# Room, order and place of loads, block inverses and output weights around a gated-delta-rule loop

## The chip, the cores and the metric

The kernel runs on one core of a Trainium2 chip, in one launch, all in float32 (products on the TensorE are taken as three products of split operands, high by high, high by low and low by high). The metric is the device time in microseconds (us) of one execution; less is better. Engines are called PE (TensorE), DVE (VectorE), ACT (ScalarE), POOL (GpSimd) and SP (SyncE, which here only issues DMAs).

## The reference

One layer of a hybrid decoder trunk, 1024 positions, width 1024. The mixer runs three branches on one projection of the normed input, and its output goes through `w_out`; cross attention to a memory of 256 rows and an MLP follow:

```
h = rms_norm(x, norm_mix); proj = h @ w_in
qkv, z, a_g, b_g, c_q, c_kv, k_idx, w_idx, ug = split_cols(proj, IN_SPLITS)
y_a = gdn_mixer(qkv, z, a_g, b_g, ...)      # conv over 4 taps, silu, gated delta rule, norm * silu(z)
y_b = dsa_mixer(c_q, c_kv, k_idx, w_idx, ...)  # index scores, top 256 of them, attention on these
y_c = conv_mixer(ug, ...)                   # depthwise conv over 31 taps, layer norm, silu
x = x + concat([y_a, y_b, y_c]) @ w_out
x = x + memory_cross_attention(rms_norm(x), rms_norm(mem), ...)
x = x + square(relu(rms_norm(x) @ w1)) @ w2
```

The gated delta rule is computed in chunks. For each chunk a unit lower triangular matrix I + A is inverted (`triangular_solve` in the reference); then a scan over the chunks carries a state S: `v_new = u - w S`, `o = q S + (qk) v_new`, `S = S * decay + k^T v_new`.

## The kernel before

**How the order comes about.** The program is written as Python generators that are woven together by weights (`weave`, line 65): each `yield` names a cost, and the thread that has had the least of its share is asked next. From the program and a model of durations a planner then fixes one list of instructions for each engine and each DMA queue ahead of the run. On the chip each engine and each queue works through its own list strictly in order; semaphores hold an instruction until its inputs are there and its room is free. Tiles lie in pools that are stacked from the left or the right end of the on-chip memory; a tile in a new pool waits until the last reader of what lay there is done.

**Stages.** (1) Norm, small projections, index scores. (2) `qkv_stage` (line 721) makes the q, k, v channels in 12 blocks of 128; each block's two halves are copied from PSUM by ACT, then convolved over four taps and stored to `qkv_d`. Woven into it are the search for the 256th score (`topk`: ACT and DVE count scores against a threshold, 32 rounds) and the first part of the 31-tap convolution on PE. (3) The preparation: `gdn_pre` (line 907) for chunks 0 to 7 of 128 positions makes the matrices and stores them to `gp_d`; `gdn_blocks(pool, n)` (line 980) inverts the 16 x 16 diagonal blocks of four chunks at a time on DVE, from `Ab_d` to `Xb_d`; `gdn_post` (line 1023) builds the full inverse from them on PE. It runs for chunks 0 to 3 and 4 to 7, the first call woven into the preparation and the second last in it. Beside it run the memory's norm, the K/V projection of the memory (`mem_stage`, whose results go to `kT_d` and `v_d`), the end of the search and of the convolution.

(4) The loop over chunks n = 0 to 7 (lines 1666 to 1694): `gdn_scan(n)` (stage name `gs`), `gdn_post(n + 1)` (`gi`) and a slice of `dsa_out` (`da`, `wa`), the attention on the selected positions and its part of `w_out`, are woven. `gdn_load` (line 895) brings a chunk's five matrices from HBM into a pool with two buffers, on the left; ahead of the first of these loads the program asks for KA and VS, keys and values of the attention. The weights `woa` of the attention's and convolution's rows of `w_out` are loaded raw into `Pm` slots, split by ACT and by DVE or POOL (`big_w_steps`, line 1221), one in each of the first four of 19 items of `dsa_out`.

(5) After the loop `out_rows` and `out_b` (`wb`) add the scan's rows of `w_out` (the weights `wb`, loaded here by the same helper into slots of `blk2`, which is opened here), `cross_q` and the rest follow (`xq`, `xp`, `xv`, `xw`), then the MLP.

**Rooms before.** On the right, in the loop: `pm` (probabilities and raw weights), `woa`, `gdnb` (the scan's `vn`, `S` and its output tiles `oc`). On the left: `gdnc` (what the inverses need), `gdnl` (the loop's loads), `dsa`. After the loop `blk` begins on the left, `blk2`, `xl` and others on the right, over these.

Of the kernel before, what the change touches and what calls it, by code (L numbers as in the profile page):

```python
# [32 lines left out]
P = 128  # L33
T = 1024
# [16 lines left out]
class Block:  # L51
# [187 lines left out]
    def mem_stage(self, wu, mp):  # L239
# [12 lines left out]
        def keys(g):  # L252
            pt = self.mm_ps([P, 2, 2, P])
            for h in range(2):
                for t in range(2):
                    nc.tensor.transpose(pt[:, h, t], kn[g][:, t, h], self.ident)
            kt = [mp.tile([P, 2, 256], F32R, name=f"kvt{i}") for i in range(2)]
            self.split(kt[0], kt[1], pt.rearrange("p h t c -> p h (t c)"))
            for i in range(2):
                nc.sync.dma_start(self.kT_d[i, :, 2 * g:2 * g + 2], kt[i].bitcast(F32))  # L260

        for g in range(4):
# [24 lines left out]
            else:  # L287
# [3 lines left out]
                for i in range(2):  # L291
                    nc.sync.dma_start(self.v_d[i, :, :, (g - 2) * 256:(g - 1) * 256], vt[i].bitcast(F32))
            if g >= 2:
# [428 lines left out]
    def qkv_stage(self, wu, wp, hT):  # L722
# [14 lines left out]
        for i in range(12):  # L737
# [7 lines left out]
            acc = wp.tile([P, T], F32, name="acc", bufs=2)  # L745
            tmp = wp.tile([P, T], F32, name="xtap", bufs=1)
            for d, x, j in ((acc, xb[:, 3:], 3), (tmp, xb[:, 0:T], 0)):
                nc.scalar.activation(d, x, AF.Copy, scale=self.cw[:, j, i:i + 1])
            nc.gpsimd.tensor_add(acc, acc, tmp)
            for d in range(1, 3):  # L750
                nc.vector.scalar_tensor_tensor(acc, xb[:, 3 - d:3 - d + T], self.cw[:, 3 - d, i:i + 1], acc,  # L751
                                               op0=OP.mult, op1=OP.add)
# [142 lines left out]
    def gdn_load(self, pool, n, c):  # L895

        for i, nm in enumerate(("vb", "kd", "qE", "qkT")):
            c[nm] = pool.tile([P, H, P], F32, name="l" + nm, bufs=2)
            self.nc.sync.dma_start(c[nm].rearrange("p h c -> p (h c)"), self.gp_d[n, i])
        c["kT"] = pool.tile([P, H, P], F32, name="lkT", bufs=2)  # L900
        self.nc.sync.dma_start(c["kT"], self.qkv_d[n, :, H:2 * H, :])
# [295 lines left out]
    def dsa_out(self, dp, pmp, wap, KA, VS, NEGM, wa, fw):  # L1197
# [3 lines left out]
        for i in range(len(items) + 3):  # L1201
# [6 lines left out]
            yield from self.weave(*ths)  # L1208
            if i < 4:
                next(fw)  # L1210
# [51 lines left out]
    def out_load(self, pool, t):  # L1262
        ya = pool.tile([P, 512], F32, name="yai", bufs=2)
        gz = pool.tile([P, H, P], F32, name="gz", bufs=2)
        q = self.nc.gpsimd if t < 2 else self.nc.sync
        q.dma_start(ya, self.ya_d[t])
        self.row_load = q.dma_start(gz, self.gz_d[t])
        return ya, gz
# [309 lines left out]
    def run(self):  # L1578
# [85 lines left out]
        ts.close()  # L1664
        wus.close()
        with ExitStack() as bs:
# [12 lines left out]
            wout = A["w_out"][0].rearrange("(k p) n -> p k n", p=P)  # L1679
            wa = []  # L1680
# [18 lines left out]
        with ExitStack() as bs:  # L1699
# [9 lines left out]
            oT, h3, y3 = {}, {}, {}  # L1709
            blk2 = bs.enter_context(sb_pool(tc, "blk2", bufs=4, side="right"))  # L1710

            def slot2(name="wslot"):
                return blk2.tile([P, 2, 1024], F32R, name=name, tag="blk2")

# [4 lines left out]
            with ExitStack() as xs:  # L1719
                xas = xs.enter_context(ExitStack())  # L1720
                xl = xas.enter_context(sb_pool(tc, "xl", bufs=1, side="right"))
                xbs = xas.enter_context(ExitStack())
                self.xt, xe, wr, xq = (xbs.enter_context(sb_pool(tc, x, bufs=1, side="right")) for x in ("xt", "xe", "wr", "xq"))
                xp = xl
                self.xl, self.xq = xl, xq
                def raw():
                    return wr.tile([P, 1024], F32, name="wraw", bufs=2)

# [15 lines left out]

                g2 = xp.tile([P, D], F32, name="g2")
                rows = {i: self.out_load(xe, i) for i in range(2)}
                nc.sync.dma_start(g2, bass.AP(tensor=A["norm_cross"].tensor, offset=A["norm_cross"].offset, ap=[[0, P], [1, D]]))
                wb, wq = [], []
# [14 lines left out]
                for i in range(NT + 6):  # L1763
# [18 lines left out]
                    if i == 9:  # L1782
                        wo = self.big_w(slot2, raw2, A["xa_wo"][0].rearrange("(k p) n -> p k n", p=P), H, D)
                        g3 = xp.tile([P, D], F32, name="g3", tag="g2")
                        nc.sync.dma_start(g3, bass.AP(tensor=A["norm_mlp"].tensor, offset=A["norm_mlp"].offset, ap=[[0, P], [1, D]]))
# [66 lines left out]
```

## Time and profile before

| | us |
|---|---|
| median of 3 runs | 1598.34 (1595.43 to 1599.29) |
| profiled execution | 1596.08 |
| its span | 1594.30 |
| PE busy | 1500.4 |
| DVE busy | 1113.8 |
| ACT busy | 739.3 |
| POOL busy | 286.0 |

The span goes from the first to the last instruction. The mean granted clock of PE is 0.973 of full speed. In the 40 slices of the page PE shows 9 (90% or more) nearly everywhere; the slices below 8 are the first one (6), the one from 359 to 399 us (7) and the one from 518 to 558 us (4). Busy times say how long an engine works, not whether anyone waits for it; that is read from the waits, the order of time and the stretches.

### The profile page before, as it was taken

Reading aid. Unit: us, or ns where it says so; the run is one execution under the profiler, and the core shown is the slowest. Engines: PE = TensorE matmul, PEld = TensorE weight load, DVE = VectorE, ACT = ScalarE, POOL = GpSimd, SP = SyncE. Lnnn points to the kernel's source line nnn. Section 1 sums busy time; section 2 is a strip of 40 time slices with the busy share of each in tenths; the row PEclk is TensorE's granted clock in tenths of the full one; section 3 lists DMA queues with packets and bytes.
Section 4 is the critical chain, followed back from the end, with each engine's and each line's share of the span. In section 5 each row is a group of like instructions: output and inputs, shape, how many; then the busy total and the mean of one; then the engine's idle time right before and its main releaser. Section 6 shows DMA issues by size and latency. Waiting matters only on the chain.

```text
span 1594.3 us, 20703 instructions
## 1 busy us (share of the span) xinstructions
PE 1500.4 (94%) x7561; PEld 1257.0 (79%) x7561; DVE 1113.8 (70%) x2056; ACT 739.3 (46%) x1381; POOL 286.0 (18%) x270
## 2 busy tenths in 40 slices
PE   6999999997999489999889998999999999999999
PEld 5977887786888378988668886888888888888887
DVE  6648667875655666775557779996579647865783
ACT  4535788768543165674334533532233233313331
POOL 4021444343953231121300200000000000000000
PEclk9999999999999799999999999999999999999999
DMA  6130222122474675434712347923641464147202
GB/s 212 38 106 14 56 84 79 54 66 75 148 250 148 224 255 163 143 104 143 257 67 67 119 172 277 361 80 131 233 171 53 158 224 163 36 158 264 79 13 94
DMA packets 125141, 220.82 MB, mean 139 GB/s; under 512 B 16246, under 2 KB 65135, under 8 KB 117871
## 3 DMA queue, kind: packets, MB, share of 16 engines
q1 hardware_dynamic: 123502, 214.25, 39.0%
q0 software_dynamic: 1536, 5.24, 0.9%
q8 instruction: 60, 0.98, 0.2%
q14 instruction: 43, 0.34, 0.1%
HBM read 158.65 MB, written 60.82 MB: 138 GB/s over the span
## 4 chain that ended last, share of the span: by engine, by line
PE 66%; DVE 10%; ACT 10%; issue 6%; DMA 4%; POOL 4%; SPq 0%; POOLq 0%; ACTq 0%; DVEq 0%
PE mlp_mm L134 6%; PE mlp_mm L135 6%; PE mlpg_mm L135 6%; PE mlpg_mm L134 6%; PE mlp_mm L133 6%; PE mlpg_mm L133 6%; ACT junka L592 4%; DVE acc L751 1%; PE gi_mm L1049 1%; PE xq_mm L133 1%; PE xw_mm L135 1%; PE xw_mm L133 1%; PE xw_mm L134 1%; PE xq_mm L134 1%; PE xq_mm L135 1%
## 5 line engine op out<-in xcount | busy, mean ns | idle before, releaser
L1475 ACT CAST wm<-wq 128x2048 fp32r<-128x2048 f32 x32 | 61.0, 1907 | 209.1 <-PE mlpg_mm L134 117.0
L134 PE MATMUL mlpg_mm<-bm,wm 128*128 128x512 f32 x256 | 101.4, 396 | 3.2 <-DVE rs_x L156 3.2
L135 PE MATMUL mlpg_mm<-bm,wm 128*128 128x512 f32 x256 | 101.6, 397 | 0.0
L134 PE MATMUL mlp_mm<-wm,am 128*128 128x512 f32 x256 | 101.2, 396 | 0.0
L135 PE MATMUL mlp_mm<-wm,am 128*128 128x512 f32 x256 | 101.2, 395 | 0.0
L133 PE MATMUL mlpg_mm<-bm,wm 128*128 128x512 f32 x256 | 99.3, 392 | 0.8 <-ACT bm L1475 0.8
L133 PE MATMUL mlp_mm<-wm,am 128*128 128x512 f32 x256 | 99.3, 396 | 0.0
L1475 ACT CAST wm<-wsum 128x2048 fp32r<-128x2048 f32 x24 | 45.8, 1907 | 105.0 <-PE mlp_mm L134 64.9
L1476 DVE TENSOR_TENSOR wm<-wq,wm 128x2048 fp32r<-128x2048 f32 x32 | 73.3, 2290 | 27.2 <-ACT wm L1475 27.2
L1476 DVE TENSOR_TENSOR wm<-wsum,wm 128x2048 fp32r<-128x2048 f32 x24 | 54.9, 2287 | 50.1 <-ACT wm L1475 50.1
L133 PE MATMUL qkv_mm<-hT,whi 128*128 128x512 f32 x192 | 76.9, 401 | 1.8 <-ACT xb L743 1.8
L1573 DVE TENSOR_TENSOR xacc<-xacc,mlp_mm 128x512 f32<-128x512 f32 x64 | 43.4, 683 | 49.1 <-PE mlp_mm L135 49.1
L134 PE MATMUL mlp_mm<-bm,wm 128*128 128x512 f32 x192 | 75.4, 393 | 1.3 <-DVE bm L1476 1.3
L133 PE MATMUL mlpg_mm<-wm,am 128*128 128x512 f32 x192 | 75.9, 396 | 0.0
L134 PE MATMUL mlpg_mm<-wm,am 128*128 128x512 f32 x192 | 75.9, 396 | 0.0
L135 PE MATMUL mlpg_mm<-wm,am 128*128 128x512 f32 x192 | 75.9, 396 | 0.0
L134 PE MATMUL qkv_mm<-hT,whi 128*128 128x512 f32 x192 | 75.8, 395 | 0.0
L135 PE MATMUL qkv_mm<-hT,wlo 128*128 128x512 f32 x192 | 75.6, 394 | 0.0
L135 PE MATMUL mlp_mm<-bm,wm 128*128 128x512 f32 x192 | 75.1, 394 | 0.0
L133 PE MATMUL mlp_mm<-bm,wm 128*128 128x512 f32 x192 | 74.7, 390 | 0.0
L185 POOL TENSOR_TENSOR wlo<-wraw,whi 128x1024 fp32r<-128x1024 f32 x24 | 59.6, 2482 | 10.4 <-ACT whi L182 6.3
L134 PEld LDWEIGHTS mlpg_mm<-bm,wm 128*128 128x128 f32 x256 | 48.6, 190 | 14.9 <-DVE rs_x L156 3.6
(516 smaller groups left out, 4459.0 us busy)
## 6 DMA issues: line engine op xcount, KB each, us to landing
bm<-hb_d SPq DMA_DIRECT2D x42, 1024.0 KB, 5.8
wq<-in_mlp_w SPq DMA_DIRECT2D x32, 1024.0 KB, 5.5
hb_d<-bm SPq DMA_DIRECT2D x14, 1024.0 KB, 12.0
wraw<-in_w_in SPq DMA_DIRECT2D x20, 512.0 KB, 3.8
qkv_d<-acc SPq DMA_DIRECT2D x12, 512.0 KB, 3.2
x<-in_x SPq DMA_DIRECT2D x8, 512.0 KB, 4.0
wraw<-in_xa_wkv SPq DMA_DIRECT2D x8, 512.0 KB, 4.7
xa<-in_x SPq DMA_DIRECT2D x16, 256.0 KB, 2.6
```

The costliest lines, as they stand in the source:

```text
L133: mm(out, l[0], r[0], start=start, stop=False, skip_group_check=on)
L134: mm(out, l[0], r[1], start=False, stop=False, skip_group_check=on)
L135: mm(out, l[1], r[0], start=False, stop=stop, skip_group_check=on)
L185: (lo_eng or nc.gpsimd).tensor_sub(lo[:, :n], raw[:, :n], hi[:, :n].bitcast(F32))
L592: Sc.activation(junka[:, :K], X[b], AF.Sign, bias=c, scale=-1.0, accum_out=n)
L751: nc.vector.scalar_tensor_tensor(acc, xb[:, 3 - d:3 - d + T], self.cw[:, 3 - d, i:i + 1], acc, op0=OP.mult, op1=OP.add)
L1049: mm(py[:, h], NAT[:, h], X[:, h], start=True, stop=True)
L1475: Sc.copy(w[0], x)
L1476: V.tensor_sub(w[1], x, w[0].bitcast(F32))
L1573: V.tensor_add(x, x, ps[ch, tt])
```

## The change

Five things are edited. The K/V stores of `mem_stage` go to POOL's queue. The short convolution is one pass of ACT and three of DVE in place of two of ACT, an addition on POOL and two of DVE. The second `gdn_blocks` leaves the preparation and becomes a thread of steps 0 and 1 of the loop, in the pool `gdnc`. The loop's first loads are asked for ahead of KA and VS, in two pools on the right (even and odd chunks), over the room of the search and the 31-tap convolution; `gdnb` and `woa` move to the left, and `blk2` is opened before the loop at the right end. The weights `wb` are loaded and split in items 6 to 9 of `dsa_out`, raw in `Pm` slots, in place of after the loop. Lastly the row tiles `yai` and `gz` become halves of one tile `yg`, whose room `g3` later takes, and `g2` moves to another pool.

```
 mem_stage:
-                nc.sync.dma_start(self.kT_d[i, :, 2 * g:2 * g + 2], kt[i].bitcast(F32))
+                nc.gpsimd.dma_start(self.kT_d[i, :, 2 * g:2 * g + 2], kt[i].bitcast(F32))
-                    nc.sync.dma_start(self.v_d[i, :, :, (g - 2) * 256:(g - 1) * 256], vt[i].bitcast(F32))
+                    nc.gpsimd.dma_start(self.v_d[i, :, :, (g - 2) * 256:(g - 1) * 256], vt[i].bitcast(F32))
 qkv_stage:
-            tmp = wp.tile([P, T], F32, name="xtap", bufs=1)
-            for d, x, j in ((acc, xb[:, 3:], 3), (tmp, xb[:, 0:T], 0)):
-                nc.scalar.activation(d, x, AF.Copy, scale=self.cw[:, j, i:i + 1])
-            nc.gpsimd.tensor_add(acc, acc, tmp)
-            for d in range(1, 3):
+            nc.scalar.activation(acc, xb[:, 3:], AF.Copy, scale=self.cw[:, 3, i:i + 1])
+            for d in range(1, 4):
                 nc.vector.scalar_tensor_tensor(acc, xb[:, 3 - d:3 - d + T], self.cw[:, 3 - d, i:i + 1], acc,
                                                op0=OP.mult, op1=OP.add)
 dsa_out:
-            if i < 4:
+            if i < 4 or 6 <= i < 10:
                 next(fw)
 out_load:
-        ya = pool.tile([P, 512], F32, name="yai", bufs=2)
-        gz = pool.tile([P, H, P], F32, name="gz", bufs=2)
+        yg = pool.tile([P, D], F32, name="yg", bufs=2)
+        ya, gz = yg[:, 0:512], yg[:, 512:].rearrange("p (h c) -> p h c", h=H)
 run:
-        pre = [both(0, 1), both(2, 3), self.weave((both(4, 5), 1.0), (self.gdn_blocks(gpa, 0), 0.4)),
-               self.weave((both(6, 7), 1.0), (first(0), 0.6)), self.gdn_blocks(gpa, 4)]
+        pre = [both(0, 1), both(2, 3), self.weave((both(4, 5), 1.0), (self.gdn_blocks(gpc, 0), 0.4)),
+               self.weave((both(6, 7), 1.0), (first(0), 0.6))]
...
+        blk2 = b2s.enter_context(sb_pool(tc, "blk2", bufs=4, side="right"))
...
+            gpl = [bs.enter_context(sb_pool(tc, f"gdnl{i}", bufs=1, side="right")) for i in range(2)]
             pmp = bs.enter_context(sb_pool(tc, "pm", bufs=1, side="right"))
-            wap = bs.enter_context(sb_pool(tc, "woa", bufs=1, side="right"))
-            gpb = bs.enter_context(sb_pool(tc, "gdnb", bufs=1, side="right"))
-            gpl = bs.enter_context(sb_pool(tc, "gdnl", bufs=1))
+            gpb = bs.enter_context(sb_pool(tc, "gdnb", bufs=1))
             dp = bs.enter_context(sb_pool(tc, "dsa", bufs=1))
+            wap = bs.enter_context(sb_pool(tc, "woa", bufs=1))
             self.psum(4)
+            self.gdn_load(gpl[0], 0, c[0])
+            self.gdn_load_A(gpc, 1, c[1])
...
-            fw = self.big_w_steps(wa, lambda: wap.tile([P, 2, 1024], F32R, name="woa", bufs=4),
-                                  lambda: pmp.tile([P, 1024], F32, name="Pm", bufs=5), wout[:, 4:8], 4, D)
+            fw = self.seq(self.big_w_steps(wa, lambda: wap.tile([P, 2, 1024], F32R, name="woa", bufs=4), praw,
+                                           wout[:, 4:8], 4, D),
+                          self.big_w_steps(wb, slot2, praw, wout[:, 0:4], 4, D))
             fill = self.dsa_out(dp, pmp, wap, KA, VS, NEGM, wa, fw)
-            self.gdn_load(gpl, 0, c[0])
-            self.gdn_load_A(gpc, 1, c[1])
+            blocks = self.gdn_blocks(gpc, 4)
             for n in range(NT):
                 ths = [(self.gdn_scan(gpb, n, c[n]), 6.0)]
+                if n < 2:
+                    ths.append((self.some(blocks, 3 - n), 3.0))
                 if n + 1 < NT:
-                    self.gdn_load(gpl, n + 1, c[n + 1])
+                    self.gdn_load(gpl[(n + 1) % 2], n + 1, c[n + 1])
...
-                xl = xas.enter_context(sb_pool(tc, "xl", bufs=1, side="right"))
+                xe, xl = (xas.enter_context(sb_pool(tc, x, bufs=1, side="right")) for x in ("xe", "xl"))
-                self.xt, xe, wr, xq = (xbs.enter_context(sb_pool(tc, x, bufs=1, side="right")) for x in ("xt", "xe", "wr", "xq"))
+                self.xt, xq = (xbs.enter_context(sb_pool(tc, x, bufs=1, side="right")) for x in ("xt", "xq"))
...
-                four = [slot2() for _ in range(4)]
-                ws = self.big_w_steps(wb, four.pop, raw, wout[:, 0:4], 4, D)
-                self.drain(self.some(ws, 3))
                 with tc.issue_after(self.row_load.ins):
-                    self.drain(ws)
                     self.drain(self.big_w_steps(wq, slot, lambda: blk.tile([P, 1024], F32, name="wraw", tag="blk"),
```

## Rows read from the trace of the kernel before

**Rows 1.** The page: busy us of each engine, share of the span, instructions

```profile
PE 1500.4 (94%) x7561; PEld 1257.0 (79%) x7561; DVE 1113.8 (70%) x2056; ACT 739.3 (46%) x1381; POOL 286.0 (18%) x270
```

**Rows 2.** PE's waits: waiting line, releaser, us in total, times, longest

```profile
PE gs_mm L1088 <- DMA lvb<-gp_d: 21.4, 1, 21.4
...
PE mem_mm L229 <- ACT whi L219: 8.2, 1, 8.2
...
PE wb_mm L134 <- POOL wslot L1229: 2.3, 1, 2.3
...
PE wb_mm L1277 <- DVE xr L1296: 2.1, 1, 2.1
...
PE wb_mm L133 <- ACT wslot L1228: 1.1, 1, 1.1
```

**Rows 3.** PE in order of time: start us, us, instruction, idle before and releaser

```profile
533.56 0.60 PE L256 MATMUL mkv_mm<-ident,kn 128*128 128x128 f32 x4
555.52 2.05 PE L1088 MATMUL gs_mm<-lvb,XT 128*128 128x128 f32 x8 [21.36 <-DMA lvb<-gp_d]
...
576.87 1.06 PE L1088 MATMUL gs_mm<-lvb,XT 128*128 128x128 f32 x8
```

**Rows 4.** Stretches: length, busy us (instructions) of PE, PEld, DVE, ACT, POOL, PEclk, DMA

```profile
180.00:360.00 180.00, 176.90 (x827) 146.44 (x826) 135.49 (x239) 143.79 (x278) 77.91 (x54) 0.99 0.25 72
...
505.00:545.00 40.00, 25.66 (x195) 23.51 (x194) 37.56 (x110) 14.84 (x34) 14.73 (x10) 0.87 0.48 160
...
534.16:546.00 11.84, 0.00 (x1) 0.00 (x0) 11.57 (x21) 2.58 (x3) 3.06 (x2) 0.67 0.59 200
...
560.00:600.00 40.00, 34.94 (x260) 31.29 (x258) 27.59 (x110) 28.07 (x79) 13.19 (x15) 1.00 0.74 247
620.00:700.00 80.00, 78.83 (x558) 72.32 (x558) 56.35 (x187) 49.43 (x114) 13.97 (x16) 1.00 0.42 133
750.00:778.00 28.00, 22.43 (x84) 15.84 (x83) 17.04 (x43) 11.57 (x23) 14.51 (x11) 0.88 0.88 308
```

**Rows 5.** SP's queue in order of time, loop entry: start us, us, DMA issue

```profile
544.69 0.32 SPq L1020 DMA_DIRECT2D Xb_d<-Wb  x1
545.05 1.01 SPq L1677 DMA_DIRECT2D KA<-KA_d  x2
...
547.44 0.89 SPq L899 DMA_DIRECT2D lvb<-gp_d  x1
```

**Rows 6.** The chain that ended last, entry and exit: start us, us, what

```profile
547.44 7.95 DMA lvb<-gp_d
...
757.99 5.66 DMA ya_d<-oc
...
763.78 4.67 DMA xr<-x_d
```

**Rows 7.** The block inverses' tile alone in one stretch: length, DVE busy, PEclk, DMA

```profile
526.00:546.00 20.00, 8.77 (x18) 0.76 0.47 148
```

**Rows 8.** PE in order of time, the last product that reads Y

```profile
503.06 0.39 PE L135 MATMUL cv_mm<-Y,diag 128*128 128x512 f32 x1
```

**Rows 9.** POOL in order of time, a transfer that POOL issues

```profile
542.94 0.78 POOL L1267 DMA_DIRECT2D gz<-gz_d  x1
```

**Rows 10.** Weight tiles at the exit: count, ns min/median/max, first and last start

```profile
L1228 ACT CAST wslot<-wraw x8: 1044/1048/1058, 747.7 to 761.6; 128x1024 fp32r<-128x1024 f32 x8
L1229 DVE TENSOR_TENSOR wslot<-wraw,wslot x4: 1224/1224/3205, 748.8 to 761.4; 128x1024 fp32r<-128x1024 f32 x4
L1229 POOL TENSOR_TENSOR wslot<-wraw,wslot x4: 2335/2392/2501, 749.7 to 765.6; 128x1024 fp32r<-128x1024 f32 x4
```

**Rows 11.** Tap lines of the short convolution: count, ns min/median/max, first and last start

```profile
L748 ACT ACTIVATE xtap<-xb,taps x12: 1136/1138/1149, 186.7 to 349.2; 128x1024 f32<-128x1024 f32 x12
...
L749 POOL TENSOR_TENSOR acc<-acc,xtap x12: 2366/2406/2413, 187.9 to 350.5; 128x1024 f32<-128x1024 f32 x12
...
L751 DVE SCALAR_TENSOR_TENSOR acc<-xb,taps,acc x24: 1269/1282/1602, 190.4 to 354.2; 128x1024 f32<-128x1024 f32 x24
```

More of the change, by code (lines that the diff above doesn't have):

```diff
@@ L897, in gdn_load @@
         for i, nm in enumerate(("vb", "kd", "qE", "qkT")):
-            c[nm] = pool.tile([P, H, P], F32, name="l" + nm, bufs=2)
+            c[nm] = pool.tile([P, H, P], F32, name="l" + nm)
             self.nc.sync.dma_start(c[nm].rearrange("p h c -> p (h c)"), self.gp_d[n, i])
-        c["kT"] = pool.tile([P, H, P], F32, name="lkT", bufs=2)
+        c["kT"] = pool.tile([P, H, P], F32, name="lkT")
         self.nc.sync.dma_start(c["kT"], self.qkv_d[n, :, H:2 * H, :])
@@ L1665, in run, with slot2 @@
         wus.close()
+        b2s = self.ctx.enter_context(ExitStack())
+        blk2 = b2s.enter_context(sb_pool(tc, "blk2", bufs=4, side="right"))
+        def slot2(name="wslot"):
+            return blk2.tile([P, 2, 1024], F32R, name=name, tag="blk2")
         with ExitStack() as bs:
+            gpl = [bs.enter_context(sb_pool(tc, f"gdnl{i}", bufs=1, side="right")) for i in range(2)]
             pmp = bs.enter_context(sb_pool(tc, "pm", bufs=1, side="right"))
-            wap = bs.enter_context(sb_pool(tc, "woa", bufs=1, side="right"))
-            gpb = bs.enter_context(sb_pool(tc, "gdnb", bufs=1, side="right"))
-            gpl = bs.enter_context(sb_pool(tc, "gdnl", bufs=1))
+            gpb = bs.enter_context(sb_pool(tc, "gdnb", bufs=1))
             dp = bs.enter_context(sb_pool(tc, "dsa", bufs=1))
+            wap = bs.enter_context(sb_pool(tc, "woa", bufs=1))
             self.psum(4)
+            self.gdn_load(gpl[0], 0, c[0])
+            self.gdn_load_A(gpc, 1, c[1])
             self.S = None
@@ L1679, in run, with praw @@
             wout = A["w_out"][0].rearrange("(k p) n -> p k n", p=P)
-            wa = []
-            fw = self.big_w_steps(wa, lambda: wap.tile([P, 2, 1024], F32R, name="woa", bufs=4),
-                                  lambda: pmp.tile([P, 1024], F32, name="Pm", bufs=5), wout[:, 4:8], 4, D)
+            wa, wb = [], []
+            def praw():
+                return pmp.tile([P, 1024], F32, name="Pm", bufs=5)
+            fw = self.seq(self.big_w_steps(wa, lambda: wap.tile([P, 2, 1024], F32R, name="woa", bufs=4), praw,
+                                           wout[:, 4:8], 4, D),
+                          self.big_w_steps(wb, slot2, praw, wout[:, 0:4], 4, D))
             fill = self.dsa_out(dp, pmp, wap, KA, VS, NEGM, wa, fw)
-            self.gdn_load(gpl, 0, c[0])
-            self.gdn_load_A(gpc, 1, c[1])
+            blocks = self.gdn_blocks(gpc, 4)
             for n in range(NT):
                 ths = [(self.gdn_scan(gpb, n, c[n]), 6.0)]
+                if n < 2:
+                    ths.append((self.some(blocks, 3 - n), 3.0))
                 if n + 1 < NT:
-                    self.gdn_load(gpl, n + 1, c[n + 1])
+                    self.gdn_load(gpl[(n + 1) % 2], n + 1, c[n + 1])
                     ths.append((self.gdn_post(gpc, n + 1, c[n + 1]), 8.0))
@@ L1709, in run @@
             oT, h3, y3 = {}, {}, {}
-            blk2 = bs.enter_context(sb_pool(tc, "blk2", bufs=4, side="right"))
-            def slot2(name="wslot"):
-                return blk2.tile([P, 2, 1024], F32R, name=name, tag="blk2")
             def h3_blocks(n):
@@ L1720, in run @@
                 xas = xs.enter_context(ExitStack())
-                xl = xas.enter_context(sb_pool(tc, "xl", bufs=1, side="right"))
+                xe, xl = (xas.enter_context(sb_pool(tc, x, bufs=1, side="right")) for x in ("xe", "xl"))
                 xbs = xas.enter_context(ExitStack())
-                self.xt, xe, wr, xq = (xbs.enter_context(sb_pool(tc, x, bufs=1, side="right")) for x in ("xt", "xe", "wr", "xq"))
+                self.xt, xq = (xbs.enter_context(sb_pool(tc, x, bufs=1, side="right")) for x in ("xt", "xq"))
                 xp = xl
                 self.xl, self.xq = xl, xq
-                def raw():
-                    return wr.tile([P, 1024], F32, name="wraw", bufs=2)
                 def raw2():
@@ L1743, in cross_w @@
                     y3[t] = self.cross_w(x, y, t, oT[t // 2], wo, g3)
-                g2 = xp.tile([P, D], F32, name="g2")
+                g2 = xq.tile([P, D], F32, name="g2")
                 rows = {i: self.out_load(xe, i) for i in range(2)}
                 nc.sync.dma_start(g2, bass.AP(tensor=A["norm_cross"].tensor, offset=A["norm_cross"].offset, ap=[[0, P], [1, D]]))
-                wb, wq = [], []
-                four = [slot2() for _ in range(4)]
-                ws = self.big_w_steps(wb, four.pop, raw, wout[:, 0:4], 4, D)
-                self.drain(self.some(ws, 3))
+                wq = []
                 with tc.issue_after(self.row_load.ins):
-                    self.drain(ws)
                     self.drain(self.big_w_steps(wq, slot, lambda: blk.tile([P, 1024], F32, name="wraw", tag="blk"),
@@ L1783, in run @@
                         wo = self.big_w(slot2, raw2, A["xa_wo"][0].rearrange("(k p) n -> p k n", p=P), H, D)
-                        g3 = xp.tile([P, D], F32, name="g3", tag="g2")
+                        g3 = xe.tile([P, D], F32, name="g3", tag="yg", bufs=2)
                         nc.sync.dma_start(g3, bass.AP(tensor=A["norm_mlp"].tensor, offset=A["norm_mlp"].offset, ap=[[0, P], [1, D]]))
```

## The prediction

> **What bounds the kernel now.** I read the page first. TensorE (PE) is busy for 94% of the span [rows 1], so almost everything that a change can win must come out of the 94 us in which PE stands still, and out of the stretches in which it ran at the lower of its two clock levels. The view of PE's waits, longest first, says where these are [rows 2]. One wait is far ahead: 21.4 us of the first `gs_mm` matmul (line 1088, step 0 of the scan) for the load `lvb<-gp_d`. Then come 8.2 us of `mem_mm` for ScalarE (ACT), and at the end of the loop three waits of `wb_mm`: 2.3, 2.1 and 1.1 us. (One of the size of the second is at the kernel's start, which the change does not touch.)
>
> Next I read the loop's entry closely. PE's last instruction before the loop starts at 533.56 and lasts 0.60, so PE runs dry at 534.16; the scan's first matmul starts at 555.52 [rows 3]. In the windows PE has 0.00 busy after that point, while VectorE (DVE) works 11.57 of 11.84 us up to 546 [rows 4]. SP's queue explains the order: it takes instructions one after the other, issues `Xb_d<-Wb` at 544.69, when DVE has finished the second four chunks' block inverses, then KA (545.05), and only at 547.44 `lvb` [rows 5], which lands 7.95 us later, among the other loads of the loop [rows 6]. So the wait is not one slow transfer: about 10.5 us of it are DVE's tail ahead of SP, 2.8 us SP's issues, 8 us the load.
>
> At the loop's exit the chain of work runs through two transfers, `ya_d<-oc` with 5.66 us and `xr<-x_d` with 4.67 [rows 6]: `xr` takes the room of the scan's output tiles and waits until the last of them has been stored, and beside it the first output weights are still being split.
>
> **The change, part by part.**
>
> *Loop entry.* Edits with one answer: the second `gdn_blocks` leaves the path before the loop, the loop's loads come ahead of KA and VS and lie in room that the search and the convolution gave up, and the K/V stores leave SP's queue, where they stood among these instructions. The block inverses are 8.77 us of DVE's work there [rows 7]. Of the 11.57 us that DVE works after PE ran dry [rows 4], 11.57 - 8.77 = 2.8 us are left (what lay earlier slides up), and they are the convolution's normalization and a K/V split, which the scan does not read. The loads can go out during PE's last 20 us of work: what they read was stored long before, and the convolution, whose `Y` lay in their new room, ends on PE at 503 [rows 8]. So the 21.4 us shrink to about DVE's 3. The block inverses come back inside steps 0 and 1: 8.8 us on a DVE that is busy 27.59 of 40 us [rows 4]. 12 us are free, but scan, inverses and attention all hand short DVE steps to PE; I charge a third, 3 us (bounds 0 and 8.8). With the standstill goes the low clock: the same `gs_mm` group took 2.05 us at 555.52 and 1.06 at 576.87 [rows 3]; I take 1 us. Sum: 21.4 - 3 - 3 + 1 = 16.4 us won. Bounds: 22.4 if all is hidden; 8 if the loads still start with DVE's tail, so that only some 11 us leave it and 3 are paid in the loop.
>
> *K/V stores on POOL.* Eight issues, at 0.78 us each by a POOL issue with DVE at work beside it [rows 9], are 6.2 us on POOL, which is busy 14.73 of 40 us [rows 4]. POOL takes its work in order too: a store that waits for its split holds up what is behind it, the `XT` products of the inverses among others. The stored K and V are read only after the loop, so their landing is covered; I cost the edit at 0, bounds 0 and -3 (four steps each held up by one issue).
> The Trainium skill speaks against this edit: "SBUF — State Buffer", section "SBUF: two separate sides", says that while DVE runs a two-port mode GpSimd can't write the descriptors of its own DMAs, and the page names some 620 ns alone against some 3100 ns beside a DVE copy. By it the eight would take 8 x 3.1 = 25 us of POOL, in my estimate, and `XT` would come late. The row above shows 0.78 us with DVE at work, so the trace does not bear it out here.
>
> *First output weights inside the loop.* After the loop go four loads of 512 KB, four ACT casts of 1.05 us, two DVE subtractions of 1.22 and two POOL ones of 2.39 [rows 10]. PE's waits there are 1.1 + 2.3 + 2.1 = 5.5 us [rows 2], and from 750 to 778 PE was granted 0.88 of the full clock [rows 4]: 0.12 x 28 = 3.4 us. At most 8.9 us. `xr` no longer takes the room of the scan's outputs, but that of loop loads and probabilities, which are read out with the scan's last matmuls. What is late next is the last unit of `w_q`, whose slots on the left now lie over the scan's `vn`, `S` and `oc`: its load waits for the `ya_d` store and then needs 4.7 us of transfer (as `xr`, of the same size [rows 6]), 1.05 of ACT and 2.4 of POOL. I take 6 us won (bounds 0 and 8.9).
> Inside the loop the same work lands in items 6 to 9, at about 620 to 700, where of 80 us PE is busy 78.83, ACT 49.43, DVE 56.35 and POOL 13.97 [rows 4]. It fits; but the raw weights take one of five `Pm` slots four times, so the scores run less far ahead. I charge 1 us (bounds 0 and 4, one us for each of the four loads).
>
> *Short convolution.* For each of 12 channel blocks ACT loses a pass of 1.14 us and POOL an addition of 2.41, DVE gains a pass of 1.28 [rows 11]: 13.7 and 28.9 us less, 15.4 us more. PE is busy 176.90 of 180 us in this stretch and hides nearly all; DVE rises from 135.5 to 151, ACT falls from 143.8 to 130 [rows 4]. Indirectly the search, whose counts fill ACT, may end sooner, and with it the 8.2 us of `mem_mm` [rows 2], since ACT turns to the memory's norm after the search's last signs. But each round of the search also needs DVE, which gets fuller. I take 1 us won; bounds -5 (a third of the added DVE time uncovered) and +10 (the whole wait and 2 us of low clock behind it).
>
> *Rooms of `yg`, `g2`, `g3`.* No new work: 0, bounds -2 and +1 (the short waits of this stage are of that size [rows 2]).
>
> *Sum.* 16.4 + 0 + 6 - 1 + 1 + 0 = 22.4 us. The profiled execution took 1596.08 us (span 1594.30 and 1.78 around it); the median of the runs is 1598.34, 2.3 above. 1596.08 - 22.4 = 1573.7; I say 1574.
>
> **Rivals.**
> 1. *Half of the entry only.* For: DVE is busy 37.56 of 40 us from 505 to 545 [rows 4], so it is nearly the bound of the whole stretch, and the moved 8.8 us are wanted soon after. Against: 12 free us in the steps that follow. Then 8 in place of 16.4: 1582, and with a poor exit up to 1590.
> 2. *The search ends early too.* For: its rounds are ACT's, and ACT sheds 13.7 us. Against: DVE is in each round as well. The memory's norm is then ready when PE asks: 10 us instead of 1, so 1565; with the whole exit and all of the entry hidden some 1556.
> 3. *The loads block SP (slower).* The new loads wait for room. If they stand in SP's queue well before the last `cv_mm` has read `Y` at 503 [rows 8], the stores and loads of the scan's preparation stand behind them, and as PE's order is fixed, PE stops too. Up to 22.4 us of such a block only eat the gain; from 27 us on (loads in the queue by 476) the kernel is slower by over 0.3%. With 32 us: 1606. For: each queue's order is worked out beforehand, by durations that need not be the chip's. Against: the preparation comes ahead of the loop in the program, so SP's queue holds it first.
> 4. *It doesn't do what it says.* The scan's first matmul finds another late thing (a PSUM bank of the convolution's norm, KA behind the loads), and the moved work costs in the loop what it saves: 1595. For: the banks change hands at this very place. Against: DVE is done with them within 3 us.
>
> **How the numbers follow.** Forecast 1574 (its own range 1566 to 1580): 0.48. Rival 1: 0.22. Rival 2: 0.16. Rival 3: 0.08. Rival 4: 0.06. No change means within 0.3%, 4.8 us, which is about what a measurement of this kernel tells from none. Faster: 0.48 + 0.22 + 0.16 = 0.86; same 0.06; slower 0.08. The range runs from 1558 (rival 2 with nearly the whole exit) to 1590 (rival 1 with a poor exit); outside are rivals 3 and 4 and the ends of 1 and 2, nearly 2 in 10.
>
> **What would show it.** Right: the first `gs_mm` starts within 5 us of the last `mkv_mm` transpose, PE waits for `lvb` under 3 us, SP issues `lvb` before the last K/V store; in the loop's first 40 us DVE is over 0.8 busy and PE's waits sum to under 8 us; `wb_mm` has no wait for `wslot`, and `xr` is loaded within 5 us of the scan's last matmul; PE is as busy as before from 180 to 360. Wrong: a PE wait over 8 us at the entry, for DVE or a DMA; a wait of `xq_mm` for `wslot` in place of the exit's; SP standing for room before 505; a longer stretch from 180 to 390.

## Result: slower by 0.6%

The changed kernel takes 1606.74 us (1604.49 to 1611.95, 5 runs) against 1598.34 (1592.63 to 1599.29, 5 runs) for the kernel before; the ratio is 1.0064, interval 1.0047 to 1.0080. The forecast was 1574, its range 1558 to 1590. The profiled execution took 1607.88 us, its span is 1606.2.

The span by stages, from first and last instructions in PE's list (us). Below, the *scan* or recurrence is `gs`, the *loop* goes from its first to its last matmul, the *exit* from there to the first `mlpg_mm`, and the *search* is the attention of `dsa_out` inside the loop, from the last `mkv_mm` to the last `da_mm` (not `topk`).

| stage | before | after | difference |
|---|---|---|---|
| start to last `qkv_mm` | 332.7 | 329.1 | -3.6 |
| to last `z_mm` | 58.0 | 65.0 | +7.0 |
| to last `mkv_mm` | 143.5 | 143.4 | 0 |
| to first `gs_mm` | 21.3 | 3.5 | -17.8 |
| to last `gs_mm` | 194.2 | 218.6 | +24.4 |
| to first `mlpg_mm` | 209.7 | 205.5 | -4.2 |
| to the end | 634.9 | 641.1 | +6.2 |

So the entry was won and the loop gave it back, with more. The page's first line, which answers to [rows 1]: PE has as many instructions and 5 us more of busy time, ACT and POOL are relieved.

```profile
PE 1505.5 (94%) x7561; PEld 1260.6 (78%) x7561; DVE 1121.0 (70%) x2068; ACT 726.5 (45%) x1369; POOL 259.6 (16%) x266
```

PE's waits (waiting line, releaser, us in total, times, longest), against [rows 2]: the 21.4 us for `lvb` and the three waits of `wb_mm` are gone (one of 1.6 us for the row tile `yg` is new), `mem_mm` stayed, and in their place stand a wait of `gi_mm` for a K/V split, one of `xq_mm` for the queries' normalization, one of `z_mm` and several small ones of the loop for ACT.

```profile
...
PE mem_mm L229 <- ACT whi L219: 7.5, 1, 7.5
PE gi_mm L1037 <- DVE kvt L145: 7.1, 1, 7.1
PE xq_mm L1326 <- DVE xqc L1319: 5.8, 2, 4.2
PE z_mm L133 <- ACT zt L671: 4.3, 1, 4.3
PE gs_mm L1085 <- issue: 3.5, 1, 3.5
PE gi_mm L1058 <- ACT X L1054: 3.4, 4, 1.6
...
PE da_mm L1180 <- ACT pth L144: 3.0, 3, 1.8
```

PE in order of time at the entry, against [rows 3]: `gs_mm` starts 4 us after the last transpose, and then PE stands once more.

```profile
536.89 0.60 PE L256 MATMUL mkv_mm<-ident,kn 128*128 128x128 f32 x4
540.95 1.72 PE L1085 MATMUL gs_mm<-lvb,XT 128*128 128x128 f32 x8 [3.46 <-issue]
549.78 1.08 PE L1037 MATMUL gi_mm<-ident,XT 128*128 128x128 f32 x4 [7.11 <-DVE kvt L145]
```

SP's queue, against [rows 5]: `lvb` and KA go out 41 and 14 us earlier. `Xb_d` of the second inverses does not: it is issued at 549.06, later than before.

```profile
506.56 0.32 SPq L896 DMA_DIRECT2D lvb<-gp_d  x1
...
530.72 0.97 SPq L1682 DMA_DIRECT2D KA<-KA_d  x2
...
549.06 0.32 SPq L1017 DMA_DIRECT2D Xb_d<-Wb  x1
```

Stretches of the loop (length, busy us of PE, PEld, DVE, ACT, POOL, granted clock, DMA), against [rows 4]: from 600 to 680 PE is busy 73.49 us; before, the same 80 us have 78.93. After, then before:

```profile
541.00:600.00 59.00, 42.48 (x281) 38.22 (x282) 41.49 (x122) 32.08 (x88) 14.77 (x16) 0.88 0.52 172
600.00:680.00 80.00, 73.49 (x503) 66.09 (x502) 52.42 (x166) 46.98 (x106) 16.63 (x17) 0.98 0.51 158
```

```profile
600.00:680.00 80.00, 78.93 (x554) 71.92 (x555) 55.20 (x179) 48.44 (x120) 12.58 (x15) 1.00 0.48 150
```

### The profile page after: what moved, and what is told of

It reads as the page before. It is cut to its first block, busy times and chain, and to the rows that moved or that the text cites. A ratio compares the mean times of both kernels' runs of the same rounds, so it can differ in the third digit from the quotient of the medians.

```text
span 1606.2 us, 20709 instructions
## 1 busy us (share of the span) xinstructions
PE 1505.5 (94%) x7561; PEld 1260.6 (78%) x7561; DVE 1121.0 (70%) x2068; ACT 726.5 (45%) x1369; POOL 259.6 (16%) x266
## 4 chain that ended last, share of the span: by engine, by line
PE 73%; DVE 11%; ACT 7%; DMA 5%; issue 3%; POOL 1%; SPq 0%; DVEq 0%; ACTq 0%; POOLq 0%
PE mlp_mm L134 7%; PE mlp_mm L135 7%; PE mlp_mm L133 6%; PE mlpg_mm L134 6%; PE mlpg_mm L133 6%; PE mlpg_mm L135 6%; ACT junka L592 3%; PE qkv_mm L133 1%; PE qkv_mm L134 1%; PE qkv_mm L135 1%; DVE acc L748 1%; PE cv_mm L135 1%; PE cv_mm L133 1%; PE cv_mm L134 1%; PE xq_mm L133 1%
## 5 line engine op out<-in xcount | busy, mean ns | idle before, releaser
L134 PE MATMUL mlp_mm<-bm,wm 128*128 128x512 f32 x192 | 76.7, 400 | 2.8 <-DVE bm L1473 2.8
L133 PE MATMUL mlp_mm<-bm,wm 128*128 128x512 f32 x192 | 76.3, 398 | 0.0
L135 PE MATMUL mlp_mm<-bm,wm 128*128 128x512 f32 x192 | 75.7, 397 | 0.0
```

Of the source, the lines that this page charges most:

```text
L133: mm(out, l[0], r[0], start=start, stop=False, skip_group_check=on)
L134: mm(out, l[0], r[1], start=False, stop=False, skip_group_check=on)
L135: mm(out, l[1], r[0], start=False, stop=stop, skip_group_check=on)
```

## The experiments

Each run stands beside runs of the kernel before on its chip; ratios are to those. The kernel before has medians of 1596.4 to 1599.2 us on these chips, so a difference of two medians from different chips is good to some 3 us. Stage numbers are from one profiled execution each.

### Which edit costs the time

**e1: the weights after the loop again**, all else as changed.

```
-            if i < 4 or 6 <= i < 10:
+            if i < 4:
                 next(fw)
...
+                ws = self.big_w_steps(wb, four.pop, lambda: wr.tile([P, 1024], F32, name="wraw", bufs=2), wout[:, 0:4], 4, D)
```

> Edit: the changed kernel with the first output weights loaded and split after the loop again. Theory A (the weights' casts stand in ACT's list behind late loads and hold up the loop): from the scan's first to its last matmul the loop shrinks from 218.6 to about 208 us, the exit gets some 5 us longer, the whole comes to about 1601. Theory B (the new rooms and the new order of the loads cost the loop its time, whatever the weights do): the loop stays at 216 to 220 and the whole at 1607 to 1612, since the exit loses its 4 us as well. Theory C (any edit reshuffles the lists; no part carries the loss): a loop anywhere between 195 and 220, with waits in other places.

1590.65 us, ratio 0.9955 (0.9933 to 0.9976): 16.1 us less by the medians (17 by the ratios, 13.4 between the two profiled executions). The search takes 191.1 us in place of 205.5, and the time from the last `gs_mm` to the first `mlpg_mm` 205.0 in place of 205.5: with four loads, casts and subtractions back at the exit, the exit is no longer, though PE waits 5.6 us there for `wslot`.

```profile
PE wb_mm L133 <- ACT wslot L1225: 4.3, 2, 2.4
...
PE wb_mm L134 <- POOL wslot L1226: 1.3, 1, 1.3
```

**e2: the short convolution in two passes of ACT, one addition and two of DVE**, as before.

> Edit: the changed kernel with the short convolution as before (two passes of ACT, POOL's addition, two of DVE). If the convolution caused the 3.3 us lost up to the end of the z products (-3.6 in the q, k, v stage, +7.0 in the z stage), the z products end at about 391 instead of 394 and the whole comes to about 1603. If it is neutral, 1606. The loop should not change under theory A (218) and is not told by B.

1604.92, ratio 1.0047 (1.0031 to 1.0064): 1.8 us less, and the intervals overlap. The stage of `z_mm` takes 56.5 us, not 65.0, that of `qkv_mm` 0.8 us more and that of `mkv_mm` 3.1. The search takes 197.3 us in place of 205.5, though nothing in it was edited.

**e3: the rooms and the early loads alone**; weights, inverses, convolution and K/V stores as before.

> Edit: loads first and the new rooms alone; block inverses, weights, short convolution and K/V stores as before. Theory A: the entry's wait of 21.4 falls to some 11, the loop stays near 194 to 200, the whole is 1588 to 1593. Theory B: the loop takes 210 or more, the whole 1603 to 1608.

1586.05, ratio 0.9918 (0.9890 to 0.9946): the fastest of all that ran, and faster than the kernel before. From the last `mkv_mm` to the first `mlpg_mm` it takes 412.0 us; before 425.2, changed 427.6. Of the 13.2 us won on the kernel before, the entry gives 18.9 and the exit 6.9, and the loop takes 12.6 back: half of what the loop lost in the changed kernel comes with the rooms and early loads alone, and what takes it is not shown.

**e4: the second block inverses pinned**: their first DVE instruction is held behind step 0's copy of S.

```
+            with (self.tc.issue_after(self.S0.ins) if pin and i == 1 else ExitStack()):
                 V.tensor_mul(t, Wv[:, :, 0:i, 0:i], Av[:, :, None, 0:i, i].to_broadcast([N, 4, i, i]))
```

> Edit: the changed kernel with one order edge more: the first DVE instruction of the second block inverses is listed behind the copy of S in step 0. In the changed kernel the planner still listed them ahead of the scan (530 to 549 us). Theory A (they, not the loads, now hold up the entry): the 7.1 us wait of PE for a K/V split goes, step 0 of the loop shrinks from 37 to about 27 us, the whole comes to about 1598. Theory B: the entry moves but the loop loses it again, 1605 or more.

1605.51, ratio 1.0045 (1.0027 to 1.0063). The 7.1 us wait falls to 2.7, and step 1's `gs_mm` starts as late as before the pin (577.7 and 578.4): the time is paid in the loop. The search takes 196.9 us.

**e8: the second block inverses before the loop again.**

> The changed kernel with the second run of block inverses back before the loop, as in the kernel before; all else as changed. The rooms alone left 2.4 us between the last mkv matmul and the first gs matmul with the blocks before the loop, so by theory A the blocks were never on the path that the loads set, and moving them back is worth minus 3 to plus 1 us: 1603.5 to 1607.5. Rival (the prediction's own step): the 3 us of blocks return to the entry, 1608 to 1611.

1606.83, ratio 1.0067 (1.0050 to 1.0083): no difference. In the changed kernel they had not moved: DVE's list has them before the loop still (start us, us), between the convolution's normalization and the K/V split for which PE waits.

```profile
541.67 1.02 DVE L1010 TENSOR_TENSOR Tb<-Ab,Wb 128x512 f32<-128x512 f32 x1
...
544.87 0.68 DVE L1012 TENSOR_REDUCE Pb<-Tb 128x64 f32<-128x512 f32 x1
545.58 2.73 DVE L1013 TENSOR_TENSOR Tb<-Wb,Pb 128x512 f32<-128x512 f32 x1
548.34 0.69 DVE L1015 TENSOR_REDUCE Wb<-Tb 128x64 f32<-128x512 f32 x1
548.95 0.68 DVE L145 TENSOR_TENSOR kvt<-mkv_mm,kvt 128x512 fp32r<-128x512 f32 x1
```

**e18: the rooms alone, and the K/V stores issued by POOL.**

> The rooms and early loads alone, with the K and V stores of the memory's second half issued by GpSimd as in the changed kernel. The prediction's step has them at 0 (bounds 0 and minus 3): 1583 to 1587. By the difference of the runs so far (e1 less rooms 4.6 us, convolution 1.8, blocks about 0) they would cost 2 to 3 us: 1587 to 1590.

1592.86, ratio 0.9970 (0.9957 to 0.9983): 6.8 us slower than e3 by the medians, more than either expected, and 2.5 between the profiled executions; the fastest run of e18 is slower than the slowest of e3. The search takes 195.0 us in place of 187.5. The eight issues take 0.54 to 0.91 us each; the two longest, merged in POOL's list, and one at the entry:

```profile
507.19 1.65 POOL L292 DMA_DIRECT2D v_d<-kvt  x2
...
533.31 0.69 POOL L292 DMA_DIRECT2D v_d<-kvt  x1 [1.02 <-ACT kvt L144]
```

In the traces DVE's order has changed: in e3 the last K/V split (`kvt`) stands ahead of the inverses' long product, in e18 behind it, and `gi_mm` waits 7.1 us for it, not 4.2. With the first `gs_mm` 1.1 us later that is 4.0 us; the rest is open. DVE of e3, then of e18:

```profile
543.70 0.67 DVE L145 TENSOR_TENSOR kvt<-mkv_mm,kvt 128x512 fp32r<-128x512 f32 x1
544.29 2.27 DVE L1016 TENSOR_TENSOR Tb<-Wb,Pb 128x512 f32<-128x512 f32 x1
```

```profile
541.13 2.73 DVE L1016 TENSOR_TENSOR Tb<-Wb,Pb 128x512 f32<-128x512 f32 x1
543.90 0.69 DVE L1018 TENSOR_REDUCE Wb<-Tb 128x64 f32<-128x512 f32 x1
544.51 0.68 DVE L145 TENSOR_TENSOR kvt<-mkv_mm,kvt 128x512 fp32r<-128x512 f32 x1
```

### Where the weights inside the loop cost 16 us

Changed kernel and e1 have the same lists up to 607 us, and from 575 on they are within 0.3 us of each other. Then ACT of the changed kernel comes to the cast of a raw weight that has not landed (start us, us, idle before and releaser), and its list holds everything behind the cast:

```profile
608.02 1.05 ACT L1225 CAST wslot<-Pm 128x1024 fp32r<-128x1024 f32 x1 [0.55 <-DMA Pm<-in_w_out]
...
613.16 1.05 ACT L1225 CAST wslot<-Pm 128x1024 fp32r<-128x1024 f32 x1 [0.54 <-DMA Pm<-in_w_out]
...
633.92 1.04 ACT L1225 CAST wslot<-Pm 128x1024 fp32r<-128x1024 f32 x1 [2.44 <-DMA Pm<-in_w_out]
634.87 0.82 ACT L1149 ACTIVATE Pm<-Pm,dm 128x640 f32<-128x640 f32 x1
```

PE waits for that last activation; from 630 to 640 it is busy 5.78 us, and from 640 to 650 its granted clock is 0.83 in the mean:

```profile
635.75 0.98 PE L1171 MATMUL da_mm<-ident,Pm 128*128 128x128 f32 x7 [1.74 <-ACT Pm L1149]
```

```profile
630.00:640.00 10.00, 5.78 (x41) 4.72 (x41) 7.84 (x29) 7.43 (x17) 1.83 (x3) 1.00 0.76 221
640.00:650.00 10.00, 10.00 (x55) 9.23 (x56) 2.55 (x8) 4.65 (x9) 3.04 (x2) 0.83 0.24 86
```

These waits are short, though: 0.55, 0.54, 2.44 and none, 3.5 us for the four casts. By the activations of `Pm` the search is 1.5 us behind e1's at 612 us and 6.0 behind at 628, and the one cast between waited 0.54. In this stretch PE runs 24 output-row matmuls (`wa_mm`) nearly in one piece ahead of the next score product; in e1 that product stands in their middle. Changed kernel, then e1:

```profile
623.44 0.39 PE L1139 MATMUL da_mm<-KA,QAb 128*128 128x512 f32 x1
```

```profile
615.00 0.39 PE L1139 MATMUL da_mm<-KA,QAb 128*128 128x512 f32 x1
```

Three edits tried to take this apart: **e5** splits each weight one search item after its load (which also spreads the four loads over items 5 to 12, in place of 6 to 9), **e6** has six `Pm` slots, **e7** issues the loads on POOL's queue.

```
 e5, dsa_out and big_w_steps:
-            if i < 4 or 6 <= i < 10:
+            if i < 4 or 5 <= i < 13:
...
             nc.sync.dma_start(rt.rearrange("p (s n) -> p s n", s=s), src[:, c * s:(c + 1) * s, :])
+            if late:
+                yield 1.0
             nc.scalar.copy(t[:, 0], rt)
 e6:
-            pm = pmp.tile([P, T], F32, name="Pm", bufs=5)
+            pm = pmp.tile([P, T], F32, name="Pm", bufs=6)
```

> The changed kernel, with each of the four weights that it splits inside the loop split one search item after its load is issued, not in the same one; the loads stay at items 5 to 12. Theory A (ScalarE's list is in order, and the cast in it waits for a load that SyncE issues late, behind its stores and the loop's own loads): the load has an item, some 10 us, to land, the casts wait for nothing, and most of the 16.1 us that undoing the weights gave comes back: 1591 to 1599. Theory B (the raw weight takes one of the five Pm slots, and the search's rows wait for a slot): the slot is held an item longer, so nothing comes back or it is up to 4 us slower: 1606 to 1611. Theory C (the added work alone, 4 casts of 1.05 us and 4 subtractions of 1.22 and 2.36 us, pushes the search back): same work, 1604 to 1608.

> The changed kernel with six Pm slots in place of five. Theory A (late load on SyncE's queue): the load is late for other reasons than a slot, 1603 to 1607. Theory B (slots short): the sixth slot is the one that the weight takes, and most of the 16.1 us comes back: 1591 to 1597. Theory C (the added work alone): 1604 to 1608.

> The changed kernel with the loads of the four weights that are split inside the loop issued by GpSimd, past SyncE's stores and loads. Theory A: the load no longer stands behind SyncE's waiting stores (x_d waited 26.3 us there between 560 and 700 us), but it stands in GpSimd's list instead, which is idle for four fifths of the loop: 1592 to 1601. Theory B (slots short): 1604 to 1608. Theory C (the added work alone): 1604 to 1608.

1604.63, 1607.92 and 1606.44 (ratios 1.0060, 1.0077, 1.0064, each within 0.0023): by the time alone, A and B both fell. By the stages the search shrinks from 205.5 us to 194.4 (e5) and 196.9 (e6), and is 206.3 in e7. That does not show the cast or the slot to be the cause: e2 and e4 left both as they were and have 197.3 and 196.9; e5's casts still wait for their loads, 4.5 us in all, and e7's wait only 1.3 beside the long search. What lengthens the search in the changed kernel stays open. ACT of e5:

```profile
595.49 1.04 ACT L1227 CAST wslot<-Pm 128x1024 fp32r<-128x1024 f32 x1 [2.43 <-DMA Pm<-in_w_out]
...
617.05 1.05 ACT L1227 CAST wslot<-Pm 128x1024 fp32r<-128x1024 f32 x1 [0.65 <-DMA Pm<-in_w_out]
...
639.42 1.04 ACT L1227 CAST wslot<-Pm 128x1024 fp32r<-128x1024 f32 x1 [0.64 <-DMA Pm<-in_w_out]
...
664.73 1.05 ACT L1227 CAST wslot<-Pm 128x1024 fp32r<-128x1024 f32 x1 [0.80 <-DMA Pm<-in_w_out]
```

And wherever the search is shorter with the weights still inside it, what follows takes it back: from the last `da_mm` to the first `mlpg_mm` it takes 231.8 and 232.5 us in e5 and e6, 235.1 and 231.6 in e2 and e4, where the changed kernel takes 222.1 and e1 226.2. So the question became what takes it back.

PE of e5 shows where: between the matmuls of the last recurrence step (751.02, 754.65, 759.90) stand some 3 and 4 us of output rows (`wb_mm`), whose weights are now ready, and `gs_mm` ends at 761.6, as in the changed kernel (759.6) and not as in e1 (750.2).

```profile
751.02 0.38 PE L1085 MATMUL gs_mm<-lvb,XT 128*128 128x128 f32 x2
...
754.65 0.38 PE L1085 MATMUL gs_mm<-lvb,XT 128*128 128x128 f32 x2
...
755.77 0.39 PE L135 MATMUL wb_mm<-wslot,yT 128*128 128x512 f32 x1
...
756.70 0.60 PE L1276 MATMUL wb_mm<-ident,yg 128*128 128x128 f32 x4
759.90 0.38 PE L1104 MATMUL gs_mm<-vn,lqkT 128*128 128x128 f32 x2
```

Then PE lacks these rows where they would cover the first queries: its waits of `xq_mm` for `xqc` sum to 10.7 us (changed 5.8, e1 3.1).

```profile
PE xq_mm L1328 <- DVE xqc L1321: 10.7, 3, 4.8
```

The other suspect was the query weights. Their four loads are issued at 766.6 to 782.4 us in the changed kernel, where before they went at 747.2 to 753.3 and in e1 at 752.8 to 770.1; from the first transposes of `xq_mm` to those of `xqc` PE takes 26.3 us with 77 output-row matmuls between (e1: 19.1 us and 48). **e9** issues them on POOL's queue, **e10** adds e5's late split, **e12** is the rooms alone with the weights inside the loop and split late, **e11** is e12 with the loads on POOL.

> The changed kernel with the four loads of the query weights (in_xa_wq), which after the loop stand in SyncE's list behind the rows' stores and loads, issued by GpSimd. Theory D (with the output weights gone from this place, the planner lists the query weights' loads later: 766.6 to 782.4 us, where the kernel with the weights after the loop has them at 752.8 to 770.1; ScalarE's casts wait 9.2 us for them, and from the first xq transpose to the first xqc transpose it is 26.4 us where it was 19.2): that stretch falls to 19 to 22 us and the time by 4 to 7 us, to 1599.5 to 1603. Rival E (TensorE idles there because the output rows that would fill it are already done): the stretch and the time stay, 1605 to 1608.

> The changed kernel with both: each weight split one search item after its load inside the loop, and the query weights' loads issued by GpSimd. The late split alone shortened the search (last mkv matmul to last da matmul 205.5 us changed, 194.4 split late, 191.1 with the weights after the loop) and the time after it took that back (222.1, 231.8 and 226.2 us). Theory D: with the query weights earlier the search's gain is kept: 1594 to 1600. Rival E (nothing fills TensorE after the loop): 1603 to 1607.

> The rooms and the loop's early loads as changed, and the output weights inside the loop, split an item late, with the query weights' loads issued by GpSimd; the block inverses, the short convolution and the K and V stores as before. By theory D the weights inside the loop then cost at most 4 us against the rooms alone (1586.05), and may give 3: 1583 to 1590. Rival (added work in the search has its price wherever it is split): 1592 to 1600.

> As e11_rooms_late_pool, but with the query weights' loads on SyncE as in the changed kernel. By theory D it keeps the long stretch before the first xqc transpose (26 to 27 us): 1597 to 1603. Rival E: the same as e11_rooms_late_pool within 2 us.

1610.22, 1608.00, 1601.18 and 1593.50 (ratios 1.0072, 1.0060, 1.0024 and 0.9983). e9 and e10 did not test D: in POOL's list the loads came later still (e9: 772.0 to 786.1), and the time got no shorter. e12 gained on e11 where D had it lose. Beside the rooms alone (e3) the weights inside the loop, split late, cost 7.5 us in e12.

**e13** to **e16** gave the loads early room: the search's pool lowest on the left, the recurrence's above it, so that the query weights' slots lie over the search's room.

```
-            gpb = bs.enter_context(sb_pool(tc, "gdnb", bufs=1))
             dp = bs.enter_context(sb_pool(tc, "dsa", bufs=1))
             wap = bs.enter_context(sb_pool(tc, "woa", bufs=1))
+            gpb = bs.enter_context(sb_pool(tc, "gdnb", bufs=1))
```

> The changed kernel with the order of three pools on the left side turned: the search's (dsa) lowest, then woa, then the recurrence's (gdnb), where the changed kernel has gdnb, dsa, woa from the bottom. The slots into which the query weights are loaded after the loop then lie over the search's room, free at 743 us, and not over the recurrence's, free at 760 us. Theory F (the query weights are late because of that room, and the time after the loop starts with them): their four loads are issued before the last recurrence step ends, the first xq to the first xqc transpose falls from 26.4 us to about 20, and the time to 1597 to 1602. Rival E (TensorE has nothing left to fill that stretch, since the output rows run earlier): the loads go early and the stretch stays over 25 us, 1605 to 1609.

> Both the search's room below and the late split of the weights inside the loop. Theory F: the search's 11 us and the query weights' 6 us add up, 1589 to 1597. Rival E: 1603 to 1607.

> The rooms and early loads, the output weights inside the loop and split an item late, the search's room below; blocks, convolution and K/V stores as before. Without the room it took 1593.5. Theory F: 6 us less, 1583 to 1589. Rival E: 1591 to 1596.

1613.91 (e13, ratio 1.0093), 1602.94 (e14, 1.0028), 1599.20 (e16, 1.0004), and 1603.05 for e15 (e3 with the same room, 1.0023; at most 1592 was expected). e15 is slower than e3 well beyond the intervals; e13 and e16 are slower than their kernels with the room as it was, and e14 1.7 us faster, with intervals that overlap. With this room the weights inside the loop, split late, cost nothing that can be told from none: e16 is 3.9 us faster than e15, and the intervals overlap. F got its stretch, 21.2 us in e13, and lost more ahead of it: ACT and POOL now have the query weights' casts in front of the first output row's, and PE waits 9.8 us there.

```profile
PE wb_mm L133 <- ACT yT L1278: 9.8, 1, 9.8
```

**e17** is e5 with one more line: the first output row's matmuls are held in PE's list behind the recurrence's last.

```
+            with (self.tc.issue_after(self.last_gs.ins) if t == 0 else ExitStack()):
                 for k in range(H):
                     self.mm3(ps, ...)
```

> e5_split_late with the first output row's matmuls held in TensorE's list behind the last recurrence matmul (the late split is kept). Theory G (the loss after the search is one of order: output rows taken early delay the recurrence, and are then missing where the first queries' normalisation has to be covered): the recurrence ends 5 to 9 us earlier, at 752 to 757 us, the waits of xq for xqc fall from 10.7 to about 6 us, and the time to 1595 to 1601. Rival (the work after the loop is the same in any order, and the late query weights alone set it): 1603 to 1606.

1595.62, ratio 0.9981 (0.9966 to 0.9995): theory G, with all three of its figures. `gs_mm` ends at 752.4, the waits for `xqc` are 5.8 us, and from the last `da_mm` to the first `mlpg_mm` it takes 221.9 us.

```profile
752.01 0.39 PE L1104 MATMUL gs_mm<-vn,lqkT 128*128 128x128 f32 x2
752.15 0.48 PE L133 MATMUL wb_mm<-wslot,yT 128*128 128x512 f32 x1
```

```profile
PE xq_mm L1329 <- DVE xqc L1322: 5.8, 2, 4.2
```

With the split late and the rows held, 11.1 of the 16.1 us are back, with the same loads, casts and subtractions in the loop: the added work itself is not the cost. The rows were not held without the late split, so what each of the two edits gives alone is known for the late split only (2.1 us, not told from none). The last 5 us are open; 3.3 of them are a longer search (194.4 against 191.1 us).

## Why the prediction was wrong

*The step that failed* is the weights inside the loop: "It fits; but the raw weights take one of five `Pm` slots four times [...] I charge 1 us (bounds 0 and 4", with 6 us won at the exit. Measured by e1, the two together cost 16.1 us. Busy sums [rows 4] said that ACT had room for four casts, and it has: e17 does the same work in the loop and is 11.1 us faster. What the sums leave out is the order. The lists are fixed and taken in order, and with the four weights in them they come out otherwise: the score product of the search behind output rows, and, once the search is shorter, output rows ahead of the recurrence's last matmuls (e17 against e5, 9.0 us). The slots, which the prediction named, are not shown to be the cost (e6 gains nothing), and why the changed kernel's search is 14 us longer than e1's stays open.
The other half, the exit, was refuted: `wb_mm`'s waits for `wslot` went as forecast, and nothing came of it. e1 still has 5.6 us of them, yet its exit is 205.0 us against 205.5. Of the 4.2 us by which the exit did shrink none needs the weights: e3's is 202.8.

*Loop entry*: the mechanism was right for the rooms. `gs_mm` came within 5 us and `lvb` cost nothing. That e3 shows 13.2 us less from the last `mkv_mm` to the first `mlpg_mm`, where 16.4 were forecast with bounds 8 and 22.4, is partly luck: 18.9 at the entry, 12.6 lost in the loop, where 3 were charged for the inverses, and 6.9 won at the exit. In the change itself it was half true: the second `gdn_blocks` "leaves the path before the loop" in the program and stayed in DVE's list, so the standstill split in two, 3.5 and 7.1 us, which is near rival 1. The "PE wait over 8 us at the entry, for DVE", named as the sign of a wrong step, came as 7.1. The 2.8 us of DVE's work that were to be left also mix two windows: the 8.77 us of [rows 7] are from 526 to 546, and from 534.16 on, where the 11.57 us were read, the same tile's instructions take 5.46. The other 3.3 hung on earlier work sliding up, and no run shows that, since the inverses stayed.

*K/V stores on POOL*, "I cost the edit at 0, bounds 0 and -3": mis-sized, 6.8 us by e18 against e3 (2.5 in the profiled executions). The parts are not additive, though: e1, which has these stores with the convolution and the inverses, is only 4.6 us slower than e3. The issues took 0.54 to 0.91 us each beside a busy DVE. The prediction's estimate from the Trainium skill ("SBUF — State Buffer", section "SBUF: two separate sides") put 3.1 us on each; the sign came out, for a reason that this trace does not show. What the page measures is a transfer beside a DVE copy, and there was no copy among the DVE instructions beside these issues, so no run here tests the rule.

*Short convolution*, +1 forecast: -1.8 by e2, not told from 0. The sign named for it, a longer stretch from 180 to 390, came: `z_mm` ends 3.4 us later than before, and 7.8 earlier again in e2.

*Rooms*: 0 forecast; they are within e3. *The query weights late*, named as what comes next at the exit and priced at 2.9 us: they came 19 to 29 us later, as a change of PE's order, and e13 shows that earlier loads alone don't help.

The rivals were each built on one wait. Rival 4 came nearest, with moved work that costs in the loop what it saves, at 0.06 and 1595; none was that work moved into a full loop makes the fixed lists of four engines come out otherwise. The 8% for "slower" stood on another mechanism, SP blocked for room, which did not happen (`lvb` at 506.56).

Open: the 6.2 us after the first `mlpg_mm`. The variants take 635 to 641 us there, the one profile of before 634.9.

## What to carry to other kernels

Free time on an engine does not price work that is moved into a tight loop: the same four casts cost 16.1 us in one order of the lists, 5 in another (e17 against e1), and nothing that could be told in a third (e16 against e15). A shorter stage is not a gain, either, until what follows it has been read: the search came out 8 to 11 us shorter in e2, e4, e5 and e6, and not one of the times is more than 2.1 us shorter. Where a planner writes the lists, an edit in the program's order may move nothing (the inverses) and an edit of a queue may move something else (the K/V split), so read the new lists, not the edit. And work that is done earlier is gone from where it covered something: hold it back if it does not end the path.

## What was not expected of the hardware

In e14 a short DVE step of the recurrence's normalization took 2.30 us, where its like take 0.16: a POOL subtraction of a weight ran from 752.68 to 755.10, and the step ended with it. DVE, then POOL:

```profile
752.82 2.30 DVE L162 SCALAR_TENSOR_TENSOR rs_t<-rs_t,rs_x 128x4 f32<-128x4 f32 x1
755.16 0.16 DVE L163 SCALAR_TENSOR_TENSOR rs_y<-rs_t,rs_i 128x4 f32<-128x4 f32 x1
```

```profile
752.68 2.42 POOL L1228 TENSOR_TENSOR wslot<-wraw,wslot 128x1024 fp32r<-128x1024 f32 x1 [8.78 <-ACT wslot L1227]
```

The Trainium skill ("SBUF — State Buffer", section "SBUF: two separate sides") says that a DVE operation with two inputs in SBUF and a POOL operation that reads SBUF shut each other out for a whole instruction. The rows agree: so a split on POOL costs not only its own 2.4 us but can also hold short steps of DVE that a recurrence waits for.
